# One more gate pair as block products, one gate fewer in the first phase, another order of units and of the steps at the border

## The chip, the cores and the metric

The kernel runs on one core of a Trainium2 chip. The metric is the device time of one execution in microseconds. The engines are named as in the profile: PE (TensorE, matmuls), PEld (its weight loads), DVE (VectorE), ACT (ScalarE), POOL (GpSimd), SP (SyncE, which issues the DMAs). Each engine works through a queue of its own; semaphores order them among one another.

## What is computed

One layer of a hybrid encoder on 1040 tokens (16 meta tokens and 1024 of the input) of width 1024, all in float32. The part that the change touches is the combined input projection and what follows from it:

```python
h = rmsnorm(h_res, norm1_w[l])
proj = h @ w_in[l]
(q, k, v, z, b_raw, a_raw, sc_b, sc_c, sc_x, gate_a, gate_b) = jnp.split(proj, SPLIT_POINTS, axis=-1)
o_dn = gated_deltanet_bidir(q, k, v, z, b_raw, a_raw, ...)
y_a = o_dn @ w_branch_dn[l]
y_b = (sc_b * depthwise_conv_centred(sc_c * sc_x, sc_conv_w[l])) @ w_branch_sc[l]
merged = jax.nn.sigmoid(gate_a) * y_a + jax.nn.sigmoid(gate_b) * y_b
```

`gated_deltanet_bidir` works on 8 heads: a short convolution on q, k and v, norms, for every chunk of tokens the inverse of a triangular matrix, and a scan over the chunks in both directions. A gated norm with silu(z) follows. Behind the merge come an output projection, and a SwiGLU block of width 2816.

## The kernel before

**Products.** Every float32 operand is kept as a high part (ACT copies it to the reduced type, `split`, L100 to L102) and a low part (DVE subtracts). A dense product of a 128-column unit of weights with 512 tokens is 8 blocks x 3 matmuls (high-high, high-low, low-high) = 24 matmuls of 128x512 (`dense`, L129). Where two units and two halves of the tokens are taken together, a scheme of seven block products in place of eight is used (`pair`, L1525): sums of weight blocks (`sums`, L1414) are multiplied with sums of token blocks T1 to T4 (`moving_sums`, L1442), each product being 12 matmuls (`product`, L1434).

**First phase** (L251 to L1395). The order of every engine's instructions is written out by hand: the program is traced under `tc.manual_schedule()` by a planner that keeps a modelled clock for each engine (the dictionary T). PE's base load is a sequence of *units*, each a 128-column block of the projection: q, k and v of each head (`u_qkv`), the three parts of a short-convolution block (`u_short`), gates (`u_gate`), z (`u_z`). `pick` (L973) chooses the unit two places ahead. A head's k, q, v are preferred where `qkv_ok` allows them (head h needs scan h-3 to be over; v also needs scan h-2 to have begun); otherwise the next *fill* is taken from `fill_units`: eight gates (four blocks j of gate A and gate B), five z units, then eight triples of short-convolution units. When the second or third unit of a triple is next (`mid`), it is taken whatever `qkv_ok` says. Between a unit's matmuls the planner puts in the steps of four streams: decay, norm, inverse, scan. Only one head at a time is in each stream, and the second part of an inverse and a scan hold a lock that excludes the other. DVE's convolutions, forward substitutions and norms come from three lanes (`pump`).

A scan (`g_scan`, L785) copies the values of its head into the tile vS (L808, one buffer), runs 8 steps, norms the sums in NP, and transposes them into a bank. ACT copies that into NP (L951, two buffers) and SP stores it to o_d (L953).

**Border** (L1481 to L1605). Under a second manual schedule, for DVE and PE only (L1484), come the last three z units (heads 5, 6, 7; `z_rows`, two halves of 24 matmuls each, tanh on ACT, a combination on DVE at L1495), the sums T1 to T4 in four steps of a generator (each ends with `split`, a cast by ACT and a subtraction by DVE of 128x2048), and the first pair. Instructions of a manual engine keep the written order among themselves; the framework's scheduler may put later instructions, from outside the block, between them. ACT's order, and SP's, are the scheduler's. The written order is the first part of `moving_sums`, then the weights of z6, z5's first half, and so on (the removed lines of the diff show it). The first pair's results leave their banks through ACT copies (L1534, L1546, L1548) and DVE additions (L1409 is the line of `add`), and products 3, 5 and 7 of a pair accumulate in the bank that product 1 began.

**After it** come the other three pairs, branch B's and branch A's projections, the merge, the output projection and the SwiGLU block, of which nothing is changed. The pairs' weights take two large tiles in turn (mB, mA); the p_d blocks are staged in the one that the last pair doesn't use (L1612).

Of the kernel before, what the change touches and what calls it, by code (L numbers as in the profile page):

```python
# [16 lines left out]
P = 128  # L17
# [7 lines left out]
H = 8  # L25
# [1 line left out]
FF = 2816  # L27
NF = FF // P
ZH = 5
GH = 4  # L30
EPS = 1e-6
NEG = -1e30

OQ, OK, OV, OZ, OBA, OSB, OSC, OSX, OGA, OGB = (
    0, 1024, 2048, 3072, 4096, 4128, 5152, 6176, 7200, 8224)


def unit(col):

    return (col if col < OBA else col - 32) // P  # L40
# [8 lines left out]
def encoder_layer(ctx: ExitStack, tc: tile.TileContext, x, meta, norm1_w, w_in, w_ba,  # L49
                  dn_conv_w, A_log, dt_bias, dn_norm_w, sc_conv_w, w_bdn, w_bsc,  # L50
                  w_out, norm2_w, w_gu, w_down, final_w, out):
    nc = tc.nc
# [12 lines left out]
    def uid(s):  # L65
        cnt["n"] += 1
        return f"{s}_{cnt['n']}"
# [29 lines left out]
    def transpose(dst, src, n=P):  # L97
        nc.tensor.transpose(dst, src, ident[:n, :n])

    def split(hi, lo, src):  # L100
        nc.scalar.copy(hi, src)  # L101
        nc.vector.tensor_tensor(out=lo, in0=src, in1=hi.bitcast(F32), op=ALU.subtract)  # L102
# [11 lines left out]
    def staged(shape):  # L114
        return *wtiles(shape), rawtile(shape)

    def wload(src, j):
        wh, wl, raw = staged([P, KT, P])
        nc.sync.dma_start(raw, src[j])
        split(wh, wl, raw)  # L120
        return wh, wl
# [56 lines left out]
    def sub(out, a, b):  # L178
        nc.vector.tensor_tensor(out=out, in0=a, in1=b, op=ALU.subtract)
# [91 lines left out]
    def pe(ns):  # L271
        T["pe"] += ns
        return T["pe"] + HOP

    def V(n, kind=0):
        return on("dve", (68 + 1.042 * n, 130 + 1.042 * n, 130 + 0.52 * n)[kind])

    def A(n):
        return on("act", 144 + 0.834 * n)
# [175 lines left out]
    def u_gate(j, dst, w):  # L455
        for i in range(2):
            po = psm()
            yield from dense_steps(po, w, hx, META + 512 * i, 512)
            th = half_buffer()
            nc.scalar.activation(th[:, :512], po, AF.Tanh, scale=0.5)  # L460
            A(512)
            nc.sync.dma_start(dst[:, 512 * i:512 * i + 512], th[:, :512])

    def u_z(h, w):

        rest = None
        for i in range(2):
            po = psm()
            for k, _ in enumerate(dense_steps(po, w, hx, META + 512 * i, 512)):
                if k == 11 and rest:  # L470
                    rest()
                yield
            th = half_buffer()[:, :512]
            nc.scalar.activation(th, po, AF.Tanh, scale=0.5)
            A(512)

            def rest(i=i, th=th, po=po):
                nc.vector.scalar_tensor_tensor(out=th, in0=th, scalar=1.0, in1=po, op0=ALU.add, op1=ALU.mult)
                V(512)
                nc.sync.dma_start(z_d[h][:, 512 * i:512 * i + 512], th)  # L480
        T["dve"] = max(T["dve"], T["act"] + HOP)
        rest()
# [302 lines left out]
    def g_scan(h, st_):  # L785
        nonlocal freed
        kq, vT, small, kn, NP, PQ, Pm = (st_[k] for k in ("kq", "vT", "small", "kn", "NP", "PQ", "Pm"))
# [4 lines left out]
        vS = dn.tile([P, 9, P], F32, tag="vS", name=uid("vS"))  # L792
        yield from take("scan")

        def newbank():
            return pss().rearrange("p (a n) -> p a n", a=4)
# [63 lines left out]
        for i in range(NC):  # L860
# [6 lines left out]
            t = pe(215 * len(act_))  # L867
# [5 lines left out]
            for d in act_:  # L873
# [4 lines left out]
                t = V(P, 1)  # L878
# [7 lines left out]
            for d in range(2):  # L886
# [3 lines left out]
                t = A(P)  # L890
# [5 lines left out]
            if i < NC - 1:  # L896
# [3 lines left out]
                t = pe(430)  # L900
# [3 lines left out]
            t2 = pe(430)  # L904
            if i < NC - 1:
                yield t
                for d in range(2):
# [6 lines left out]
                    t = V(P, 1)  # L914
# [28 lines left out]
            yield T["pe"] + 300  # L943
        yield T["dve"] + HOP
        for c4 in range(2):
            oT = NP[:, 4 * c4:4 * c4 + 4, 1 - c4]
            pt = newbank()
            for c in range(4):
                transpose(pt[:, c], oacc[4 * c4 + c])
            yield pe(430)  # L950
            nc.scalar.copy(oT, pt)  # L951
            A(512)
            nc.sync.dma_start(o_d[h][:, c4 * 512:(c4 + 1) * 512].rearrange("p (c t) -> p c t", c=4), oT)  # L953
# [5 lines left out]
                 for h in range(H) for i, off in enumerate((OK, OQ, OV))]  # L959
    fill_units = [(off + j * P, lambda w, j=j, i=i: u_short(j, i, w), None, i)  # L960
                  for j in range(8) for i, off in enumerate((OSC, OSX, OSB))]
    fill_units += [(off + j * P, lambda w, j=j, d_=d_[j]: u_gate(j, d_, w), None, None)
                   for j in range(GH) for off, d_ in ((OGA, ta_d), (OGB, tb_d))]
    fill_units += [(OZ + h * P, lambda w, h=h: u_z(h, w), None, None) for h in range(ZH)]
    fill_units = fill_units[24:] + fill_units[:24]
    done = freed = 0
    decs, norms, invs, scans = [], [], [], []

# [67 lines left out]
    with tc.tile_pool(name="st", bufs=1) as st:  # L1036
# [64 lines left out]
        def high(t, g):  # L1101
            p = size(t)
            nc.scalar.copy(hx[0][:, 4 * g:4 * g + 4, C0 + P * t:C0 + P * t + p], banks[t, g][:, :, :p])  # L1103
# [308 lines left out]
    mov = {}  # L1412
# [29 lines left out]
    def moving_sums():  # L1442

        c = [slice(C0 + META + 512 * i, C0 + META + 512 * i + 512) for i in range(2)]
        f = lambda m: m.bitcast(F32)
        h0, h1 = ([f(hx[0][:, 4 * i:4 * i + 4, cc]) for cc in c] for i in range(2))
        l0, l1, l2 = ([f(t[:, :, cc]) for cc in c] for t in low_tiles)
        for i in range(2):
            for j in range(2):
                mov[f"B{i + 1}{j + 1}"] = hx[0][:, 4 * i:4 * i + 4, c[j]], [hx[1][4 * i + k][:, c[j]] for k in range(4)]  # L1450
        for i, n in enumerate(("T1", "T2", "T3")):
            t = big(f"b{i}", [P, 2, 4, 512])
            mov[n] = t[:, 0], t[:, 1]
        x, y = (big(g, [P, 2, 4, 512], F32) for g in ("mA", "b3"))
        t1, t2, t3, d_ = x[:, 0], x[:, 1], y[:, 0], y[:, 1]
        a, b = slice(0, 2), slice(2, 4)
        sub(t1, h0[1], h0[0])
        sub(d_, l0[1], l0[0])
        add(t1, t1, d_)
        split(*mov["T1"], t1)  # L1460
        yield
        sub(t2, h1[1], t1)
        add(t2[:, a], t2[:, a], l1[1])
        add(t2[:, b], t2[:, b], l2[1])
        split(*mov["T2"], t2)
        yield
        sub(t3, h1[1], h0[1])
        sub(d_[:, a], l1[1], l0[1][:, a])
        sub(d_[:, b], l2[1], l0[1][:, b])
        add(t3, t3, d_)  # L1470
        split(*mov["T3"], t3)
        yield
        t = big("b3", [P, 2, 4, 512])
        mov["T4"] = t[:, 0], t[:, 1]
        sub(t1, h1[0], t2)
        add(t1[:, a], t1[:, a], l1[0])
        add(t1[:, b], t1[:, b], l2[0])
        split(*mov["T4"], t1)
        yield

    raw_slots.extend((tp, f"raw{i}") for i in range(2))  # L1481
    left, right = slice(0, 512), slice(512, 1024)
    border0 = ExitStack()
    border0.enter_context(tc.manual_schedule(engines={mybir.EngineType.DVE, mybir.EngineType.PE}))  # L1484
    z_units = [wload(w_in, unit(OZ + ZH * P))]

    def z_rows(h):
# [13 lines left out]
    def pair_weights(n, j):  # L1501

        s_hl[n % 2] = big(("mB", "mA")[n % 2], [P, 2, 2, KT, P])
        if n == 0:
            u = big("w2", [P, 2, 4, P])
            u_hl[0] = u[:, 0], u[:, 1]
        elif n == 1:
            u_hl[1] = [tp.tile([P, 4, P], F32R, tag="t2", name=uid("u_hl"), bufs=2) for _ in range(2)]
        gh, gl = wtiles([P, KT, P])
        rg, ru = (rawtile([P, KT, P]) for _ in range(2))  # L1510
        nc.sync.dma_start(rg, w_in[unit(OGA + j * P)])
        nc.sync.dma_start(ru, w_in[unit(OGB + j * P)])
        A_ = {"A11": (gh[:, 0:4], gl[:, 0:4]), "A12": (gh[:, 4:8], gl[:, 4:8])}

        def first():
            split(gh, gl, rg)

        def second():
            split(*u_hl[n % 2], ru[:, 4:8])
            A_["A22"] = u_hl[n % 2]  # L1520
            sums(rg, ru, rg[:, 0:4], rg[:, 4:8], ru[:, 0:4], ru[:, 4:8])
            stationary2(n, ru, rg, ru, A_)
        return A_, first, second

    def pair(n, j, A_, first, second):  # L1525
# [54 lines left out]
        return o1  # L1580

    sums_of_blocks = moving_sums()
    z0, z1, z2 = (z_rows(h) for h in range(ZH, H))
    next(sums_of_blocks)
    z_units.append(wload(w_in, unit(OZ + (ZH + 1) * P)))
    next(z0)
    next(z0)
    next(sums_of_blocks)
    z_units.append(wload(w_in, unit(OZ + (H - 1) * P)))
    next(z0)  # L1590
    pair0 = pair_weights(0, GH)
    next(z1)
    pair0[1]()
    next(z1)
    pair0[2]()
    next(z1)
    next(z2)
    next(sums_of_blocks)
    next(z2)
    next(sums_of_blocks)  # L1600
    next(z2)
    for n, j in enumerate(range(GH, KT)):
        o1 = pair(n, j, *(pair_weights(n, j) if n else pair0))
        if n == 0:
            border0.close()  # L1605
# [5 lines left out]
    for j in range(KT):  # L1611
        pr = mg[GH % 2 == 0][:, j] if j < 4 else s4(SEQ) if j < 6 else rawtile([P, SEQ])  # L1612
        nc.sync.dma_start(pr, p_d[j])
# [47 lines left out]
    mov = {n: (b_hl[:, 2 * i], b_hl[:, 2 * i + 1]) for i, n in enumerate(("B11", "B21"))}  # L1661
# [84 lines left out]
    t = KT - 1  # L1746
# [229 lines left out]
```

## Time and profile before

| what | value |
|---|---|
| three timed runs, median (lowest to highest) | 2003.53 us (2002.02 to 2005.52) |
| the profiled execution, its own time | 2004.27 us |
| its span, first to last instruction | 2002.5 us |
| mean granted PE clock | 0.995 |
| head 0's first chunk of values to the last head's output store | 214.0 to 951.9 us |
| last fill's last DVE instruction (L451) | 970.4 us |
| first pair's first product (L1440) | 1009.3 us |
| HBM read, written | 180.67 MB, 68.25 MB |

The page of the profile gives busy times and the costliest groups; its lists of waits say who waited for whom; the windows give each engine's busy time, the granted clock and the DMA share of a stretch; the timeline lists instructions with the idle time ahead of them in brackets and what ended it. PE's matmuls overlap in the records: a 128x512 one is shown with some 390 ns while the next starts some 227 ns later, so its cost is taken from starts.

### The profile page before, as it was taken

Reading aid. Unit: us, or ns where it says so; the run is one execution under the profiler, and the core shown is the slowest. Engines: PE = TensorE matmul, PEld = TensorE weight load, DVE = VectorE, ACT = ScalarE, POOL = GpSimd, SP = SyncE. Lnnn points to the kernel's source line nnn. Section 1 sums busy time; section 2 is a strip of 40 time slices with the busy share of each in tenths; the row PEclk is TensorE's granted clock in tenths of the full one; section 3 lists DMA queues with packets and bytes.
Section 4 is the critical chain, followed back from the end, with each engine's and each line's share of the span. In section 5 each row is a group of like instructions: output and inputs, shape, how many; then the busy total and the mean of one; then the engine's idle time right before and its main releaser. Section 6 shows DMA issues by size and latency. Waiting matters only on the chain.

```text
span 2002.5 us, 31873 instructions
## 1 busy us (share of the span) xinstructions
PE 1977.3 (99%) x12011; PEld 1724.1 (86%) x12011; DVE 1396.6 (70%) x3013; ACT 836.4 (42%) x1961; POOL 107.8 (5%) x407
## 2 busy tenths in 40 slices
PE   9999999999999999999999999999999999999998
PEld 8998889899999999999788888887878888888887
DVE  6887688878888888855685544469766666656575
ACT  6472465536463646333244221225323333334344
POOL 2011101010101010100000000000000000000000
PEclk9999999999999999999999999999999999999999
DMA  3123222222132222221236743123765345477654
GB/s 132 65 90 95 80 80 75 85 61 83 45 99 59 75 59 75 59 65 43 95 116 242 249 160 95 63 93 110 256 217 217 123 155 188 158 273 244 195 172 167
DMA packets 131121, 251.00 MB, mean 125 GB/s; under 512 B 45013, under 2 KB 54662, under 8 KB 128535
## 3 DMA queue, kind: packets, MB, share of 16 engines
q1 hardware_dynamic: 130391, 247.92, 37.5%
q8 instruction: 94, 1.54, 0.3%
q10 hardware_dynamic: 576, 1.05, 0.1%
q14 instruction: 60, 0.49, 0.1%
HBM read 180.67 MB, written 68.25 MB: 124 GB/s over the span
## 4 chain that ended last, share of the span: by engine, by line
PE 90%; DVE 4%; DMA 3%; ACT 1%; issue 1%; SPq 0%; DVEq 0%; ACTq 0%
PE pm L341 33%; PE pd L1440 12%; PE pe L1440 5%; PE pm L1440 3%; PE pd L903 1%; PE pd L882 1%; PE pd L866 1%; PE pe L136 1%; PE pe L134 1%; PE pd L869 1%; PE pe L135 1%; PE pe L603 1%; PE pd L134 1%; PE pd L136 1%; PE pd L135 1%; PE pe L1882 1%
## 5 line engine op out<-in xcount | busy, mean ns | idle before, releaser
L341 PE MATMUL pm<-hTh,wh 128*128 128x512 f32 (+4 forms) x1296 | 446.4, 350 | 0.3 <-ACT hTh L1103 0.2
L341 PE MATMUL pm<-al,wh 128*128 128x512 f32 (+4 forms) x1296 | 445.9, 349 | 0.0
L341 PE MATMUL pm<-hTh,wl 128*128 128x512 f32 (+4 forms) x1296 | 443.8, 348 | 0.0
L341 PEld LDWEIGHTS pm<-hTh,wh 128*128 128x128 f32 x1296 | 242.7, 188 | 13.7 <-issue 0.8
L341 PEld LDWEIGHTS pm<-hTh,wl 128*128 128x128 f32 x1296 | 242.9, 188 | 12.3 <-issue 0.4
L341 PEld LDWEIGHTS pm<-al,wh 128*128 128x128 f32 x1296 | 242.9, 188 | 12.2 <-issue 0.4
L102 DVE TENSOR_TENSOR al<-raw,ring_h 128x1024 fp32r<-128x1024 f32 x73 | 88.6, 1222 | 65.0 <-ACT ring_h L101 64.7
L101 ACT CAST ring_h<-raw 128x1024 fp32r<-128x1024 f32 x73 | 76.7, 1053 | 107.8 <-PE pd L1884 34.4
L990 DVE TENSOR_TENSOR wl<-raw,wh 128x512 fp32r<-128x512 f32 x118 | 79.5, 688 | 30.6 <-ACT wh L993 30.2
L363 DVE SCALAR_TENSOR_TENSOR kq<-ra,wc,kq 128x520 f32<-128x520 f32 x128 | 96.6, 755 | 4.8 <-ACT kq L393 3.5
L889 ACT ACTIVATE w<-pd,small 128x128 f32<-128x128 f32 x128 | 39.9, 363 | 117.1 <-PE pd L882 116.7
L101 ACT CAST wh<-raw 128x1024 fp32r<-128x1024 f32 x47 | 49.3, 1050 | 87.4 <-PE pe L135 25.5
L496 DVE TENSOR_TENSOR tm<-fP,fN 128x135 f32<-128x135 f32 (+23 forms) x248 | 72.0, 290 | 4.9
L500 DVE TENSOR_TENSOR fP<-fP,tm 128x135 f32<-128x135 f32 (+23 forms) x248 | 71.6, 289 | 5.1
L993 ACT CAST wh<-raw 128x512 fp32r<-128x512 f32 x118 | 69.2, 621 | 3.7 <-issue 3.6
L1409 DVE TENSOR_TENSOR b<-pd,b 128x512 f32<-128x512 f32 x22 | 15.2, 690 | 69.4 <-PE pd L1440 69.4
L1819 ACT ACTIVATE b<-b 128x512 f32<-128x512 f32 x22 | 13.9, 632 | 114.3 <-DVE b L1409 114.3
L102 DVE TENSOR_TENSOR wl<-raw,wh 128x1024 fp32r<-128x1024 f32 x47 | 57.3, 1219 | 3.8 <-ACT wh L101 3.7
L856 ACT ACTIVATE jk<-NP 128x128 f32<-128x128 f32 x64 | 19.9, 311 | 83.5 <-DVE NP L852 82.5
L876 DVE SCALAR_TENSOR_TENSOR r<-pd,negEG,vS 128x128 f32<-128x128 f32 x120 | 36.8, 345 | 25.7 <-PE pd L866 25.2
L1440 PE MATMUL pd<-b_hl,wh 128*128 128x512 f32 x176 | 54.5, 391 | 0.0
L912 DVE SCALAR_TENSOR_TENSOR S<-S,eGl,pd 128x128 f32<-128x128 f32 x104 | 31.6, 342 | 30.2 <-PE pd L899 29.8
(590 smaller groups left out, 4689.5 us busy)
## 6 DMA issues: line engine op xcount, KB each, us to landing
raw<-in_w_in_dram SPq DMA_DIRECT2D x72, 512.0 KB
raw<-in_w_gate_up_dram SPq DMA_DIRECT2D x44, 512.0 KB
sums<-in_w_down_dram SPq DMA_DIRECT2D x22, 512.0 KB
t_d<-sums SPq DMA_DIRECT2D x11, 1024.0 KB
raw<-s_d SPq DMA_DIRECT2D x44, 256.0 KB
raw<-t_d SPq DMA_DIRECT2D x44, 256.0 KB
act_d<-b SPq DMA_DIRECT2D x43, 256.0 KB
raw<-act_d SPq DMA_DIRECT2D x33, 256.0 KB
```

Of the source, the lines that this page charges most:

```text
L101: nc.scalar.copy(hi, src)
L102: nc.vector.tensor_tensor(out=lo, in0=src, in1=hi.bitcast(F32), op=ALU.subtract)
L134: mm(po[:m, :n], wh[:, k, :m], xhk[:, t0:t0 + n], start=(k == 0), stop=False)
L135: mm(po[:m, :n], wh[:, k, :m], xlk[:, t0:t0 + n], start=False, stop=False)
L136: mm(po[:m, :n], wl[:, k, :m], xhk[:, t0:t0 + n], start=False, stop=(k == KT - 1))
L341: mm(po[:, :n], ww[:, k], f(k)[:, t0:t0 + n], start=i == 0, stop=i == 3 * KT - 1)
L363: nc.vector.scalar_tensor_tensor(out=acc, in0=raw[:, h0 + t:h0 + t + hn], scalar=wc[:, t, col:col + 1], in1=acc, op0=ALU.mult, op1=ALU.add)
L496: nc.vector.tensor_tensor(out=tv, in0=fP[:, 0:r, j:j + 1].broadcast_to([P, r, n]), in1=fN[:, j:j + 1, j + 1:32].broadcast_to([P, r, n]), o ...
L500: nc.vector.tensor_tensor(out=fP[:, 0:r, j + 1:32], in0=fP[:, 0:r, j + 1:32], in1=tv, op=ALU.subtract)
L990: nc.vector.tensor_tensor(out=u[1][1][:, k], in0=u[2][:, k], in1=u[1][0][:, k].bitcast(F32), op=ALU.subtract)
L993: nc.scalar.copy(u[1][0][:, k], u[2][:, k])
L1440: mm(po, x[:, k], y, start=k + i == 0 and not add_to, stop=k == 3 and i == 2, skip_group_check=add_to)
```

## The change

1. `GH` goes from 4 to 3: gate block 3 (two units) leaves the fills, and five pairs are taken by the seven products.
2. The fills come in another order: three gates, the eight triples, the other three gates, the five z units.
3. A scan's transposed output is copied into vS and stored from there.
4. At the border ACT joins the engines in written order; the sums' four steps become seven, in which the low part of a sum is taken one step after its cast; z6's weights are loaded and split ahead of the first sum, and the other steps are put in other places.

```diff
@@ -27,7 +27,7 @@
 FF = 2816
 NF = FF // P
 ZH = 5
-GH = 4
+GH = 3
 EPS = 1e-6
 NEG = -1e30
 
@@ -943,7 +943,7 @@
             yield T["pe"] + 300
         yield T["dve"] + HOP
         for c4 in range(2):
-            oT = NP[:, 4 * c4:4 * c4 + 4, 1 - c4]
+            oT = vS[:, 4 * c4:4 * c4 + 4]
             pt = newbank()
             for c in range(4):
                 transpose(pt[:, c], oacc[4 * c4 + c])
@@ -962,7 +962,7 @@
     fill_units += [(off + j * P, lambda w, j=j, d_=d_[j]: u_gate(j, d_, w), None, None)
                    for j in range(GH) for off, d_ in ((OGA, ta_d), (OGB, tb_d))]
     fill_units += [(OZ + h * P, lambda w, h=h: u_z(h, w), None, None) for h in range(ZH)]
-    fill_units = fill_units[24:] + fill_units[:24]
+    fill_units = fill_units[24:24 + 3] + fill_units[:24] + fill_units[24 + 3:]
     done = freed = 0
     decs, norms, invs, scans = [], [], [], []
 
@@ -1454,34 +1454,43 @@
         x, y = (big(g, [P, 2, 4, 512], F32) for g in ("mA", "b3"))
         t1, t2, t3, d_ = x[:, 0], x[:, 1], y[:, 0], y[:, 1]
         a, b = slice(0, 2), slice(2, 4)
+        high = lambda n, t: nc.scalar.copy(mov[n][0], t)
+        low_part = lambda n, t: sub(mov[n][1], t, f(mov[n][0]))
         sub(t1, h0[1], h0[0])
         sub(d_, l0[1], l0[0])
         add(t1, t1, d_)
-        split(*mov["T1"], t1)
+        high("T1", t1)
         yield
         sub(t2, h1[1], t1)
         add(t2[:, a], t2[:, a], l1[1])
         add(t2[:, b], t2[:, b], l2[1])
-        split(*mov["T2"], t2)
+        high("T2", t2)
+        low_part("T1", t1)
+        yield
+        low_part("T2", t2)
         yield
         sub(t3, h1[1], h0[1])
         sub(d_[:, a], l1[1], l0[1][:, a])
         sub(d_[:, b], l2[1], l0[1][:, b])
         add(t3, t3, d_)
-        split(*mov["T3"], t3)
+        high("T3", t3)
+        yield
+        sub(t1, h1[0], t2)
+        low_part("T3", t3)
         yield
         t = big("b3", [P, 2, 4, 512])
         mov["T4"] = t[:, 0], t[:, 1]
-        sub(t1, h1[0], t2)
         add(t1[:, a], t1[:, a], l1[0])
         add(t1[:, b], t1[:, b], l2[0])
-        split(*mov["T4"], t1)
+        high("T4", t1)
+        yield
+        low_part("T4", t1)
         yield
 
     raw_slots.extend((tp, f"raw{i}") for i in range(2))
     left, right = slice(0, 512), slice(512, 1024)
     border0 = ExitStack()
-    border0.enter_context(tc.manual_schedule(engines={mybir.EngineType.DVE, mybir.EngineType.PE}))
+    border0.enter_context(tc.manual_schedule(engines={mybir.EngineType.DVE, mybir.EngineType.PE, mybir.EngineType.Activation}))
     z_units = [wload(w_in, unit(OZ + ZH * P))]
 
     def z_rows(h):
@@ -1581,24 +1590,27 @@
 
     sums_of_blocks = moving_sums()
     z0, z1, z2 = (z_rows(h) for h in range(ZH, H))
-    next(sums_of_blocks)
     z_units.append(wload(w_in, unit(OZ + (ZH + 1) * P)))
     next(z0)
+    next(sums_of_blocks)
+    next(sums_of_blocks)
     next(z0)
+    z_units.append(wload(w_in, unit(OZ + (H - 1) * P)))
     next(sums_of_blocks)
-    z_units.append(wload(w_in, unit(OZ + (H - 1) * P)))
     next(z0)
+    next(z1)
     pair0 = pair_weights(0, GH)
     next(z1)
     pair0[1]()
     next(z1)
     pair0[2]()
-    next(z1)
     next(z2)
     next(sums_of_blocks)
     next(z2)
     next(sums_of_blocks)
+    next(sums_of_blocks)
     next(z2)
+    next(sums_of_blocks)
     for n, j in enumerate(range(GH, KT)):
         o1 = pair(n, j, *(pair_weights(n, j) if n else pair0))
         if n == 0:
```

## The prediction

> **What bounds the kernel now.** First the head of the page, then the list of what TensorE (PE) waited for.
>
> ```profile
> span 2002.5 us, 31873 instructions
> PE 1977.3 (99%) x12011; PEld 1724.1 (86%) x12011; DVE 1396.6 (70%) x3013; ACT 836.4 (42%) x1961; POOL 107.8 (5%) x407
> PE 90%; DVE 4%; DMA 3%; ACT 1%; issue 1%; SPq 0%; DVEq 0%; ACTq 0%
> PE pe L136 <- DVE wl L102: 3.8, 1, 3.8
> ```
>
> PE is the bound: the chain that ended last runs over it for 90% of the span, and its longest single wait anywhere is 3.8 us. So only two things pay: fewer PE instructions, and holes closed. The one big hole lies where the diff works, between the first phase and the gate pairs. The chain of waits there, in order of time (start, us, what):
>
> ```profile
> 971.10 2.02 DMA p_d<-rb
> 973.24 2.29 DVE mA L179
> ...
> 980.09 1.92 ACT b L101
> 982.03 2.29 DVE b L102
> 984.32 1.15 DVE wl L102
> 985.51 0.79 PE pe L136
> 986.30 0.43 PE pe L134
> ...
> 990.88 0.23 PE pe L136
> ```
>
> The low part of head 6's z weights (984.32) stands in DVE's queue behind the three passes of T1, ACT's cast and the low part of T1. PE had started 48 matmuls of z5 at about 970.2 and two of z6, was through at 981.5, and stood until 985.51: 4.0 us. Then twelve matmuls took 0.43 us instead of 0.23, another 2.5 us. The hole costs **6.5 us**. The windows show the granted clock (the 0.50) in that stretch:
>
> ```profile
> 987.00:988.00 1.00, 1.00 (x4) 0.81 (x3) 1.00 (x1) 0.00 (x0) 0.00 (x0) 0.50 0.96 381
> ```
>
> **The change part by part.** Costs of matmuls, from a stretch that holds two gate units and nothing else, and one that holds 512-wide products throughout:
>
> ```profile
> 170.90:192.60 21.70, 21.70 (x97) 17.97 (x96) 1.00 0.30 102
> 1100.00:1200.00 100.00, 100.00 (x443) 82.81 (x442) 47.46 (x51) 20.74 (x20) 0.00 (x0) 1.00 0.59 202
> ```
>
> (a) *Three gates for four, five pairs for four.* Two dense units of 48 matmuls leave the first phase: 96 x 0.226 = -21.7 us. A fifth pair of seven products of 12 comes: 84 x 0.226 = +19.0 us. Net **-2.7 us**, if PE stays the bound on both sides. Weight loads (2 x 512 KB), stores, and the casts move from the first phase to the pairs, where DVE is busy for 47 of 100 us in the row above: hidden there. The fifth pair ends in the other large tile (mB), so the staging of p_d moves to mA, which is free as early: nothing.
>
> (b) *z weights ahead of the sums.* The low part of z6 now goes to DVE right after the last fill unit, some 2 us after z0 starts on PE, and is wanted 10.9 us after it. The hole above goes: **-6.5 us**.
>
> (c) *ACT in the written order, casts and low parts of the sums staggered.* What is late next? In before, DVE and PE follow the written order here and ACT does not:
>
> ```profile
> 1012.25 0.59 ACT L1534 COPY s<-pd 128x512 f32<-128x512 f32 x1 [1.36 <-PE pd L1440]
> ...
> 1018.23 1.92 ACT L101 CAST b<-b 128x2048 fp32r<-128x2048 f32 x1
> ```
>
> The copy at 1012.25 is written in `pair`, behind all seven steps of the sums, but ACT took it ahead of the cast of T3 (1018.23), and of T4's later still. What a written order does to such an instruction is seen on DVE:
>
> ```profile
> 1029.97 2.29 DVE L102 TENSOR_TENSOR b<-mA,b 128x2048 fp32r<-128x2048 f32 x1 [2.03 <-ACT b L101]
> ...
> 1032.77 0.68 DVE L1409 TENSOR_TENSOR s<-pm,s 128x512 f32<-128x512 f32 x1
> ```
>
> The addition at 1032.77 reads the first pair's second product (bank pm), which PE had done by 1014.8 (the rows of products below); it came 18 us later, behind the low part of T4. With ACT in the written order the copy of the first pair's first bank comes behind T4's cast, and PE's third product of that pair accumulates into the same bank, so PE waits for the copy. When? Count from z0's first matmul (0). DVE can begin T1 at about 4.0 (973.24 - 970.2 = 3.0 in before; the last fill is now a z unit, with a tanh of 0.6 ahead of its DVE pass and store). Two rows give the shorter passes (two of 1024, three of 512):
>
> ```profile
> 988.29 2.36 DVE L1409 TENSOR_TENSOR mA<-mA,al 128x1024 f32<-128x1024 f32 x2
> ...
> 1003.70 1.89 DVE L179 TENSOR_TENSOR raw<-raw,raw 128x512 f32<-128x512 f32 x3
> ```
>
> Up to T4's sum DVE has 10 passes of 2048 at 2.25, 6 of 1024 additions at 1.18, 4 low parts of 1024 at 1.15 and 10 instructions of 512 at 0.63: 22.5 + 7.1 + 4.6 + 6.3 = 40.5 us. So T4's sum is ready at 44.5, or 47.5 with three waits of about 1 us (z7's cast, a cast of the first pair's sums, one low part of the next pair's weights slipped in). Cast 1.9, copy 0.6: the bank is free at 47.0 to 50.0. PE ends six z halves at 6 x 24 x 0.227 = 32.7 and the two products ahead of the wait at 38.1. That leaves a gap of 8.9 to 11.9 us, which only products of later pairs, outside the written order, can fill. Before has such fillers:
>
> ```profile
> L1440 PE MATMUL pd<-hTh,wh x4: 389/389/389, 1009.3 to 1011.4; 128*128 128x512 f32 x4
> L1440 PE MATMUL pm<-hTh,wl x4: 389/389/389, 1012.5 to 1014.5; 128*128 128x512 f32 x4
> L1440 PE MATMUL pe<-hTh,wh x4: 388/389/395, 1020.5 to 1022.6; 128*128 128x512 f32 x4
> ```
>
> The first two rows are the first pair's own first products; the third, in another bank, is a product of the second pair pulled ahead of the first pair's T3 product. Now two such products (5.4 us) have their weights and banks in time; a third needs a low part that DVE reaches only at about 48. Left: 3.5 to 6.5 us, taken as 4.5, and 2.5 us of slow clock as in the hole above: **+7.0 us**. Its ends: 0 (four fillers, 10.9 us, cover it) and 15 (none, 11.9, and 3.4 of slow clock). In the row nearest to this wait, the 4.0 us hole, the price was 6.5, so the middle is taken.
>
> The Trainium skill, "TensorE: Matmul & The Clock Gate", section "What's actually happening", says the half rate sets in after at least one idle window of about 3.4 us; by that a new gap under 3.4 us would cost no clock, and at its lower end (+3.5) the sum would be -5.7. This trace does not hold to it: a wait of 2.05 us was also followed by the half clock.
>
> ```profile
> 1494.67 2.85 PE L1440 MATMUL pd<-b,w 128*128 128x512 f32 x8 [2.05 <-DVE b L1409]
> ```
>
> ```profile
> 1496.00:1497.00 1.00, 1.00 (x4) 0.78 (x3) 0.61 (x1) 0.00 (x0) 0.00 (x0) 0.50 0.97 393
> ```
>
> (d) *Outputs sent from vS.* vS has one buffer, so ACT's L808 of the next head now waits for the two stores; NP is free earlier.
>
> ```profile
> 883.07 1.28 SPq L953 DMA_DIRECT2D o_d<-NP  x2
> 892.85 2.35 ACT L808 ACTIVATE vS<-pd,small 16x128 f32<-16x128 f32 x9 [1.50 <-PE pd L98]
>   DMA o_d<-NP: 1.4, 1
> ```
>
> The next write comes 8.5 us after the last store was issued, and a 256 KB store took 2.0 us (971.10 above): no wait. The 1.4 us is DVE's only wait for these stores, and PE did not stop for it. **0** on the path; bounds -1.4 and, if a scan followed at once, +2.
>
> (e) *Order of the fills.* Same work, other places: the 8 x 3 short-convolution units now follow three gate units, and three gates and five z units come last. On a busy PE this is 0. It matters only through the scans, which must be over before the fills are.
>
> ```profile
> 951.20 1.12 SPq L953 DMA_DIRECT2D o_d<-NP  x2
> 492.31 2.35 ACT L808 ACTIVATE vS<-pd,small 16x128 f32<-16x128 f32 x9 [0.70 <-PE pd L98]
> 494.57 0.24 ACT L580 COPY kn<-pe 16x128 f32<-16x128 f32 x1
> 524.52 0.34 SPq L671 DMA_DIRECT2D nd<-NP  x1
> L392 ACT COPY ra<-pm x9: 403/439/481, 453.5 to 490.6; 128x336 f32<-128x336 f32 x3, 128x320 f32<-128x320 f32 x3, 128x384 f32<-128x384 f32 x3
> ```
>
> Fills went on for 19 us after the last head's output (951.2 to 970.2); with 21.7 us less of them they would end at 948.5, 2.7 us before it. So the cover is just gone unless the scans move. I think they move forward. Inversions run one at a time and set the pace; the inverse of head 4 could start only at 524.5, though scan 3, which follows the inverse of head 3, began at 492.3, because its normalisation (494.57) waited for head 4's q and k units, and these (453.5 on) had to let the first short triple finish. Put into the slots of before, the new list gives head 3's k one unit later (some 10 us, which the inversion lane still absorbs) and head 4's k one unit earlier, so that everything from head 4 on comes some 14 us earlier: last output near 937, fills until 948.5, cost **0**.
>
> Sum on the profiled execution (2004.27 us, span 2002.5): -2.7 - 6.5 + 7.0 + 0 + 0 = **-2.2 us**. The median of the three timed runs is 2003.53, so the forecast is 2001.3 us.
>
> **Rivals.** *The new ACT order costs little.* If DVE has no waits and four products are pulled ahead, PE stands for 0 to 2 us and the clock stays up: -2.7 - 6.5 + 1 = -8.2, 1995.3 us. For it: before filled the whole wait for T4 that way. Against: weights and banks for a third filler come late. *The change doesn't do what it says for PE:* no filler fits, and the gap of 11.9 + 3.4 comes whole: -9.2 + 15 = +5.8, 2009.3 us. Against: the filler row. *The scans outlast the fills (slower).* Place: the end of the first phase. A head's k may be chosen only between triples; if a scan ends just after that choice, q and k come three units, about 50 us, late. By my estimate from the starts of the units and scans in the trace, the choices for heads 4 to 7 follow the end of the scan they need by 18, 13, 16 and 9 us; one miss puts the last output at about 937 + 35 = 972 instead of 937, and PE then has 20 us of scan with half of it idle, and a slow clock: about +15 on -2.2, 2016 us. It decides from the moment the last output comes after 948.5.
>
> **How the numbers follow.** Forecast (1998.5 to 2005) 40%; cheap ACT order 28%; scans outlast the fills 22%; no fillers 10%. 0.2% is 4 us, about what a measurement can tell from no change: faster is below 1999.5, slower above 2007.5. Faster takes the 28% and a quarter of the forecast's 40%: 38%. Slower takes the last two cases, less their milder part: 29%. Same: 33%. The range, 1994 to 2012, leaves out the worse half of the scan case and the tails. The likeliest case's own range is 1998.5 to 2005.
>
> **What would show it.** The wait of L136 for L102 near z6 gone; 1200 instead of 1296 matmuls in each L341 group. Right on (c): a wait of PE in L1440 for ACT's L1534 some 40 to 50 us after z0, with a stretch of clock 0.50 behind it; wrong: products back to back through the first pair. Right on (e): the last o_d store before the last fill's evictions. Wrong: PE waiting on scan lines (L866 to L903) or L98 at the end of the first phase. What would break the forecast most is (e), since its slots are taken from the old timing.

## The result and the profile after

The changed kernel takes 2007.28 us (median of 22 runs, 2003.46 to 2011.47) against 2003.41 us before (22 runs beside them, 2000.47 to 2006.41): ratio 1.0018, 95% interval 1.0012 to 1.0025. That is slower by about 3.9 us, just inside the 0.2% that the prediction took for no difference, and on the other side of 1 than its forecast of 2001.3. The profiled execution is the fastest of the 22: 2003.46 us, span 2001.7. So a second profile of the same kernel was taken (the last of the experiments, span 2004.7); both are read here.

The head of the page of the first profile:

```profile
span 2001.7 us, 31862 instructions
PE 1974.2 (99%) x11999; PEld 1720.7 (86%) x11999; DVE 1398.8 (70%) x3020; ACT 837.2 (42%) x1964; POOL 108.0 (5%) x407
```

Cut at the start of z0 (the first L134 matmul behind the fills) and at the first L134 matmul of branch B behind the pairs, with 0.227 us for each of the 144 matmuls of the z units and the 84 of each pair that lie between them:

| | z0 starts | z0 to branch B | of it matmuls | of it holes and slow clock | branch B to the end |
|---|---|---|---|---|---|
| before | 970.2 | 115.9 | 480 x 0.227 = 109.0 | 6.9 | 916.4 |
| after | 946.0 | 142.7 | 564 x 0.227 = 128.0 | 14.7 | 913.0 |
| after, second profile | 946.6 | 144.8 | 128.0 | 16.8 | 913.3 |

The first phase became 24 us shorter, the fifth pair costs 19, and **the holes of the border doubled**. What PE waited for, from the list of waits (total, times, longest):

```profile
PE pd L1440 <- DVE s L1504: 7.7, 2, 5.9
...
PE pd L1440 <- ACT s L1543: 1.1, 1, 1.1
...
PE pd L136 <- DVE wl L102: 0.5, 1, 0.5
```

The wait of 3.8 us for z6's low part (L136 for L102) is gone; the 0.5 in the last row is for z7's. In its place stands a larger one, in the first pair. PE's timeline there (start, duration, line; in brackets the idle time ahead and what ended it):

```profile
985.12 0.39 PE L1440 MATMUL pm<-hTh,wl 128*128 128x512 f32 x1
991.38 0.77 PE L1440 MATMUL pd<-hTh,wh 128*128 128x512 f32 x1 [5.88 <-DVE s L1504]
...
996.21 0.50 PE L1440 MATMUL pd<-hTh,wl 128*128 128x512 f32 x1
998.56 0.50 PE L1440 MATMUL pd<-hTh,wh 128*128 128x512 f32 x1 [1.85 <-DVE s L1504]
998.90 0.40 PE L1440 MATMUL pd<-al,wh 128*128 128x512 f32 x1
1000.43 2.93 PE L1440 MATMUL pd<-b,mB 128*128 128x512 f32 x6 [1.14 <-ACT s L1543]
```

At 985.12 the first pair's second product ends. Its third (operands b and mB, the sums) starts at 1000.43, when ACT's copy has freed the bank. In the 15 us between them PE ran one product of a later pair (twelve matmuls, 991.38 to 996.21) and two matmuls of another. Each of these had to wait for a bank that a z unit's combination on DVE (L1504, z2's two halves) gave back. ACT, in the same stretch:

```profile
981.29 0.59 ACT L1502 ACTIVATE s<-pd 128x512 f32<-128x512 f32 x1
...
990.67 1.90 ACT L1457 CAST b<-b 128x2048 fp32r<-128x2048 f32 x1 [4.09 <-DVE b L1409]
992.48 0.59 ACT L1502 ACTIVATE s<-pd 128x512 f32<-128x512 f32 x1
998.00 1.90 ACT L1457 CAST b<-mA 128x2048 fp32r<-128x2048 f32 x1 [4.93 <-DVE mA L1409]
999.81 0.58 ACT L1543 COPY s<-pd 128x512 f32<-128x512 f32 x1
```

ACT is idle for 4.09 and 4.93 us, waiting for the sums of T3 and T4, and behind their casts stand, in the written order, z2's second tanh (992.48) and the copy of the first pair's bank (999.81; ready to run since that bank's product ended). z2's first tanh had run at 981.29. DVE, whose sums make ACT wait:

```profile
953.10 2.29 DVE L179 TENSOR_TENSOR mA<-hTh 128x2048 f32<-128x2048 f32 x1 [4.26 <-issue]
...
990.55 0.68 DVE L1504 SCALAR_TENSOR_TENSOR s<-s,pd 128x512 f32<-128x512 f32 x1
...
995.55 2.35 DVE L1409 TENSOR_TENSOR mA<-mA,al 128x1024 f32<-128x1024 f32 x2
997.83 0.68 DVE L1504 SCALAR_TENSOR_TENSOR s<-s,pd 128x512 f32<-128x512 f32 x1
...
999.03 1.22 DVE L102 TENSOR_TENSOR wl<-raw,wh 128x1024 fp32r<-128x1024 f32 x1
```

T1 begins at 953.10, 7.1 us after z0, and from there DVE has hardly a gap until T4's last addition (995.55 to 997.9). So PE, through ACT's order, hangs on the whole chain of the sums. The two combinations (990.55 and 997.83) stand behind the sums of T3 and T4 in DVE's own written order. The clock went with it (PEclk is the third figure from the end):

```profile
991.40:996.60 5.20, 5.20 (x12) 3.75 (x12) 5.20 (x3) 1.67 (x2) 0.00 (x0) 0.52 0.00 0
...
1000.40:1004.00 3.60, 3.56 (x10) 2.85 (x11) 3.60 (x4) 1.52 (x2) 0.00 (x0) 0.60 0.06 24
```

The end of the first phase, by line:

```profile
L953 SPq DMA_DIRECT2D o_d<-vS x4: 320/380/428, 861.6 to 938.0; - x4
```

```profile
L341 PE MATMUL pm<-hTh,wh x1264: 302/334/582, 17.6 to 945.3; 128*128 128x320 f32 x47, 128*128 128x384 f32 x45, 128*128 128x512 f32 x43, 128*128 128x336 f32 x29
```

The last head's output is stored at 938.0, and the fills go on to 945.3: the scans kept their cover.

### The profile page after: what moved, and what is told of

The parts are those of the page before. It is cut to its first block, busy times and chain, and to the rows that moved or that the text cites. A ratio compares the mean times of both kernels' runs of the same rounds, so it can differ in the third digit from the quotient of the medians.

```text
span 2001.7 us, 31862 instructions
## 1 busy us (share of the span) xinstructions
PE 1974.2 (99%) x11999; PEld 1720.7 (86%) x11999; DVE 1398.8 (70%) x3020; ACT 837.2 (42%) x1964; POOL 108.0 (5%) x407
## 4 chain that ended last, share of the span: by engine, by line
PE 47%; DVE 3%; ACT 1%; issue 1%; DMA 1%; SPq 0%; DVEq 0%; ACTq 0%
PE pd L1440 13%; PE pe L1440 6%; PE pm L1440 4%; PE pe L1894 1%; PE pe L1895 1%; PE pe L1896 1%; PE pd L1894 1%; PE pd L1895 1%; PE pd L1896 1%; PE pd L135 1%; PE pd L134 1%; PE pe L135 1%; PE pe L134 1%; PE pd L136 1%; PE pe L136 1%; PE pm L1895 1%
## 5 line engine op out<-in xcount | busy, mean ns | idle before, releaser
L341 PE MATMUL pm<-hTh,wh 128*128 128x320 f32 (+4 forms) x1264 | 434.2, 349 | 0.4 <-ACT hTh L1103 0.2
L341 PE MATMUL pm<-al,wh 128*128 128x320 f32 (+4 forms) x1264 | 433.6, 348 | 0.0
L341 PE MATMUL pm<-hTh,wl 128*128 128x320 f32 (+4 forms) x1264 | 431.7, 347 | 0.0
L341 PEld LDWEIGHTS pm<-hTh,wh 128*128 128x128 f32 x1264 | 236.7, 188 | 12.6 <-issue 1.3
L341 PEld LDWEIGHTS pm<-hTh,wl 128*128 128x128 f32 x1264 | 237.0, 188 | 10.9 <-issue 0.4
L341 PEld LDWEIGHTS pm<-al,wh 128*128 128x128 f32 x1264 | 236.9, 188 | 10.3
L102 DVE TENSOR_TENSOR al<-raw,ring_h 128x1024 fp32r<-128x1024 f32 x73 | 88.6, 1223 | 64.8 <-ACT ring_h L101 64.4
L102 DVE TENSOR_TENSOR wl<-raw,wh 128x1024 fp32r<-128x1024 f32 x48 | 58.5, 1220 | 13.6 <-ACT wh L101 13.4
L1440 PE MATMUL pd<-b_hl,wh 128*128 128x512 f32 x176 | 54.4, 390 | 0.0
L1440 PE MATMUL pd<-b,mB 128*128 128x512 f32 x204 | 50.7, 398 | 1.1 <-ACT s L1543 1.1
```

The lines of the kernel that those rows point to most:

```text
L341: mm(po[:, :n], ww[:, k], f(k)[:, t0:t0 + n], start=i == 0, stop=i == 3 * KT - 1)
L1440: mm(po, x[:, k], y, start=k + i == 0 and not add_to, stop=k == 3 and i == 2, skip_group_check=add_to)
```

## The experiments

The theory at the start (A): putting ACT into the written order costs what the rest of the change gains, because the first pair's bank copy stands behind T4's cast. The rival (B): the steps' new places on DVE, or the shorter first phase, make the hole, and ACT's order matters little. Each kernel is compared with runs of the kernel before on the same chip; the medians of before lay between 2003.4 and 2004.1 throughout.

**ACT out of the written order, all else as changed.**

```diff
-    ...manual_schedule(engines={...DVE, ...PE, mybir.EngineType.Activation}))
+    ...manual_schedule(engines={...DVE, ...PE}))
```

> The changed kernel with one edit: ACT is taken out of the engines in written order at the border (DVE and PE stay). Theory A (ACT's written order puts the first pair's copy L1543 behind T4's cast, and PE's wait for it costs about 15 us): the hole at z0 + 39 to 55 us shrinks to 4 us or less, time about 1996 us, 11 us under the changed kernel and some 7 under the kernel before. Theory B (the hole comes from DVE's written order: the z7 combinations L1504 stand behind T3 and T4 and hold the banks that the pulled-ahead products need): ACT's order is immaterial, the hole stays, about 2007 us.

Measured: 1993.76 us (1989.33 to 1996.87), ratio 0.9949 (0.9935 to 0.9962). z0 to branch B took 129.2 us: 1.2 of holes instead of 14.7. ACT's timeline shows the copy pulled ahead of both casts:

```profile
984.06 0.59 ACT L1543 COPY s<-pd 128x512 f32<-128x512 f32 x1 [0.94 <-PE pd L1440]
...
991.92 1.92 ACT L1457 CAST b<-b 128x2048 fp32r<-128x2048 f32 x1 [1.84 <-DVE b L1409]
...
999.25 1.92 ACT L1457 CAST b<-mA 128x2048 fp32r<-128x2048 f32 x1 [2.81 <-DVE mA L1409]
```

T4's cast is as late as in the changed kernel (z0 + 51.6 against z0 + 52.0), so DVE's chain is the same; only the pair's copies moved, the first from z0 + 53.8 to z0 + 36.4, and PE hardly stopped. A holds. This version is also the fastest of all: 0.5% under the kernel before.

**The other way round: the kernel before with ACT in the written order, nothing else.**

```diff
-    ...manual_schedule(engines={...DVE, ...PE}))
+    ...manual_schedule(engines={...DVE, ...PE, mybir.EngineType.Activation}))
```

> The kernel before with one edit: ACT joins the engines in written order at the border. Theory A: a second hole opens in the first pair, 10 to 15 us, since T4's cast comes later there than in the changed kernel (z0 + 58): about 2014 to 2019 us. Theory B: no new hole, 2003.5 us.

Measured: 2019.15 us (2017.19 to 2020.16), ratio 1.0075 (1.0062 to 1.0089): +15 us from one word. The wait, and ACT:

```profile
PE pd L1440 <- DVE s L1495: 8.6, 1, 8.6
```

```profile
1028.36 1.90 ACT L101 CAST b<-mA 128x2048 fp32r<-128x2048 f32 x1 [7.40 <-DVE mA L1409]
1030.16 0.58 ACT L1534 COPY s<-pd 128x512 f32<-128x512 f32 x1
```

The copy that stood at 1012.25 in before comes at 1030.16, and the fillers wait for z2's bank (L1495 is before's L1504). The same mechanism without any other part of the change.

**ACT in written order up to the first pair, free from there on.**

```diff
     next(sums_of_blocks)
+    border0.close()
+    border0.enter_context(tc.manual_schedule(engines={...DVE, ...PE}))
     for n, j in enumerate(range(GH, KT)):
```

> The changed kernel, with ACT in written order up to the first pair and free from there on (DVE and PE stay in written order throughout). It parts two readings of the gain from freeing ACT. If the place of the pair's copies behind T4's cast is what cost (theory A): about 1994 us, like the kernel with ACT free. If it was the written order among the z and sums steps themselves: about 2007 us, like the changed kernel.

Measured: 1996.34 us (1995.4 to 1997.72), ratio 0.9961 (0.9948 to 0.9973). Of the 0.69% between the changed kernel and the one with a free ACT, 0.57% come back by freeing ACT from the pair on alone. The rest is within the two intervals; in this profile PE has a gap of 3.03 us, 2.56 of them waiting, and slow clock behind it:

```profile
995.68 2.93 PE L1440 MATMUL pd<-b,mB 128*128 128x512 f32 x6 [2.56 <-DVE b L179]
```

```profile
995.70:999.40 3.70, 3.70 (x10) 2.97 (x11) 2.80 (x3) 1.41 (x1) 0.00 (x0) 0.58 0.02 9
```

**z2 earlier, ACT in written order.** The banks that the fillers waited for are given back before T3's sum:

```diff
     next(z2)
-    next(sums_of_blocks)
     next(z2)
+    next(z2)
     next(sums_of_blocks)
     next(sums_of_blocks)
-    next(z2)
+    next(sums_of_blocks)
     next(sums_of_blocks)
```

> The changed kernel with one difference: all three steps of z2 (head 7) are written ahead of T3, so that its two combinations on DVE and its tanh on ACT come earlier and its banks are given back some 8 us sooner; ACT keeps the written order, so the first pair's copy still stands behind T4's cast, at about z0 + 54. Theory A (the copy's place behind T4's cast makes the hole, the banks held by z2's combinations decide how many products of later pairs can fill it): two to three of them (5.4 to 8 us) run while PE waits, the holes between z0 and branch B shrink from 14.8 to 6 to 10 us, and the time is 1999 to 2004 us against 2004 of the kernel before. Rival B (the banks were the whole cause): no hole is left, about 1994 us. Rival C (weights, not banks, kept the fillers out): as the changed kernel, 2007 us.

Measured: 2006.71 us (2005.22 to 2008.01), ratio 1.0015 (1.0006 to 1.0024): rival C, and the theory's figure was wrong. The waits for L1504 are gone, and in their place stand the low parts of the next pairs' weights; in this order a row of PE's list of waits, of DVE's timeline and two of PE's:

```profile
PE pd L1440 <- DVE wl L102: 8.8, 2, 6.5
```

```profile
1000.20 1.22 DVE L102 TENSOR_TENSOR wl<-raw,wh 128x1024 fp32r<-128x1024 f32 x1
```

```profile
994.60 0.39 PE L1440 MATMUL pd<-hTh,wl 128*128 128x512 f32 x1
1001.47 0.80 PE L1440 MATMUL pd<-hTh,wl 128*128 128x512 f32 x1 [6.47 <-DVE wl L102]
```

The low part at 1000.20 stands in DVE's queue behind T4's additions; in the changed kernel it stood at 999.03. So two things kept the fillers out, banks and weights, both behind the sums on DVE, and freeing the banks shows the weights. One product and two matmuls ran in the hole either way.

**The border alone** (new border and ACT's order; four gates, the old fills and outputs).

```diff
-GH = 3
+GH = 4
-            oT = vS[:, 4 * c4:4 * c4 + 4]
+            oT = NP[:, 4 * c4:4 * c4 + 4, 1 - c4]
-    fill_units = fill_units[24:24 + 3] + fill_units[:24] + fill_units[24 + 3:]
+    fill_units = fill_units[24:] + fill_units[:24]
```

> The changed kernel's border alone (z weights in front, staggered sums, ACT in written order), with four gates, the old order of fills and outputs through NP. Theories A and B: the old hole of 6.5 us goes and one of about 15 comes: 2003.5 + 8.3 = 2011.8 us. If the loss of the changed kernel sat in the first phase: about 2003 us or less.

Measured: 2010.97 us (2008.48 to 2013.04), ratio 1.0034 (1.0022 to 1.0047), +6.9 us. Holes between z0 and branch B: 120.9 - 109.0 = 11.9 us, against 6.9 in before, with two waits for L1504 again:

```profile
PE pd L1440 <- DVE s L1504: 5.8, 2, 4.1
```

So the border loses 6.9 us by itself, whatever the first phase does.

**The fills alone** (three gates, five pairs, the new order of units, on the kernel before).

```diff
-GH = 4
+GH = 3
-    fill_units = fill_units[24:] + fill_units[:24]
+    fill_units = fill_units[24:24 + 3] + fill_units[:24] + fill_units[24 + 3:]
```

> The kernel before with three gates, five pairs and the new order of fills alone; border and outputs as before. By the profile of the changed kernel the first phase ends 24.2 us earlier and a pair costs 19.0: 2003.5 - 5.2 = 1998.3 us. Rival (the scans outlast the fills in typical runs, though not in the profiled one): 2004 us or more.

Measured: 2001.52 us (1999.0 to 2003.76), ratio 0.9988 (0.9979 to 0.9997): -2.5 us. This is 3 us less than was expected. z0 starts at 946.6, 23.6 us earlier, but T1 begins at z0 + 4.4 instead of 3.1, and the old hole grew:

```profile
PE pe L136 <- DVE wl L102: 5.7, 1, 5.7
```

**z6's weights ahead of the first sum, alone**, on the kernel before:

```diff
-    next(sums_of_blocks)
     z_units.append(wload(w_in, unit(OZ + (ZH + 1) * P)))
+    next(sums_of_blocks)
     next(z0)
```

> The kernel before with z6's weights loaded and split ahead of the first sum, and nothing else. The 6.5 us of the old hole go: 1997 us. Rival: T4 comes 1 us later and PE's wait moves into the first pair: 2000 us or more.

Measured: 2000.85 us (1999.22 to 2002.41), ratio 0.9981 (0.9972 to 0.9989): -3.3 us, half of the 6.5. The hole moved to z7's weights, for which PE waits until 995.9:

```profile
PE pd L136 <- DVE wl L102: 2.4, 1, 2.4
```

**Fills and z6's weights, without the staggered sums**, ACT free (the last two diffs together):

> The kernel with the new fills (three gates, five pairs), plus z6's weights ahead of the first sum; the sums in four steps with cast and low part together, ACT free, outputs through NP. If staggering the sums is worth nothing once the weights come first: 2001.5 - 9.3 (its hole of 6.1 and some 3 of slow clock) = 1992 us, level with the kernel with ACT free. If the staggering is needed: 1996 us or more.

Measured: 2001.06 us (1999.31 to 2005.76), ratio 0.9988 (0.9979 to 0.9997). Here the whole hole went to z7's weights:

```profile
PE pd L136 <- DVE wl L102: 6.9, 1, 6.9
```

The kernel with a free ACT is 7.3 us faster than this one. That is what the seven staggered steps are worth, together with the new places of the steps around them, which no run takes apart (the outputs from vS, the other difference, are worth nothing, below). Here DVE waits 1.98 and 1.96 us for the casts of T1 and T2, and z7's low part stands behind T2's, 20.4 us after T1's start. With the staggered steps and a free ACT it stands ahead of T2's low part, DVE doesn't wait for these casts, and it comes 14.3 us after T1's start.

**The outputs from vS alone**, on the kernel before:

```diff
-            oT = NP[:, 4 * c4:4 * c4 + 4, 1 - c4]
+            oT = vS[:, 4 * c4:4 * c4 + 4]
```

> The kernel before with the scans' outputs sent from vS, and nothing else. The prediction's 0: 2003.5 to 2004 us, no PE wait for L808 and no DVE wait for the stores of o_d. Rival (the next head's copies wait for the stores): a microsecond or two per head, 2008 us or more.

Measured: 2003.89 us (2002.6 to 2007.19), ratio 1.0004 (0.9995 to 1.0013). Nothing, as expected.

**A gate pair more** (six pairs, two gates, ACT free).

```diff
-GH = 3
+GH = 2
```

> The changed kernel with ACT taken out of the written order and one gate pair more (two gates in the first phase, six pairs). Two gate units of 48 matmuls leave the first phase (-21.7 us) and 84 come to the pairs (+19.0). Theory: the fills are also the cover of the scans. With three gates the last head's output was stored some 9 us ahead of the last fill's end; with 21.7 us less the fills end near 925, the scans near 938, and PE stands half idle for some 13 us and gets the slow clock behind it: 1993.8 - 2.7 + 8 to 20 = 1999 to 2011 us, with PE waiting on the scan's lines. Rival (the scans move forward with the fills, or other work covers them): 1993.8 - 2.7 = 1991 us and no such waits.

Measured: 1997.92 us (1996.32 to 2000.09), ratio 0.9971 (0.9959 to 0.9982): 0.2% slower than with three gates, a little under the theory's range, and by another way. PE did not stand in the scan's end: the last fill ended at 920, z0 started at 921.9 among the last scan's steps and filled them; only 0.3 us of wait is left there. The price came later. The chain of waits, DVE, and PE's list:

```profile
934.24 1.98 DMA o_d<-vS
```

```profile
936.53 2.29 DVE L179 TENSOR_TENSOR mA<-hTh 128x2048 f32<-128x2048 f32 x1 [3.33 <-DMA o_d<-vS]
...
950.79 1.22 DVE L102 TENSOR_TENSOR wl<-raw,wh 128x1024 fp32r<-128x1024 f32 x1
```

```profile
PE pd L136 <- DVE wl L102: 5.1, 1, 5.1
```

T1 had to wait for the last output's store, so the sums began 14.6 us after z0, and z7's weights behind them came late.

**The changed kernel once more.**

> The changed kernel once more, unaltered, for a second profile: the first profile was of the fastest of its executions. If the new hole is the cause, it stands again between z0 and branch B with 14 to 16 us in all, the first pair's copy comes some 54 us after z0 behind T4's cast, and the difference between the first profile (2003.5 us) and the median (2007.3 us) is slow clock behind short gaps elsewhere, in spells of 3.4 us, which come in some executions and not in others. Rival: the hole itself varies by several us from execution to execution.

Measured: 2005.40 us (2003.89 to 2008.07, 8 runs), ratio 1.0010 (1.0000 to 1.0020). The waits in the first pair are the same:

```profile
PE pd L1440 <- DVE s L1504: 7.8, 2, 5.9
...
PE pd L1440 <- ACT s L1543: 1.1, 1, 1.1
```

The two spans differ by 3.0 us: 0.6 of it arises before z0, 2.0 between z0 and branch B, 0.4 behind. In two stretches the slow clock differs; first the first profile, then the second:

```profile
986.00:1008.00 22.00, 13.63 (x41) 10.24 (x42) 20.01 (x17) 8.93 (x10) 0.00 (x0) 0.77 0.14 53
1384.00:1404.00 20.00, 16.54 (x62) 11.80 (x61) 18.11 (x23) 8.37 (x10) 0.00 (x0) 0.91 0.49 159
```

```profile
986.00:1008.00 22.00, 13.05 (x33) 9.39 (x33) 19.94 (x17) 8.28 (x9) 0.00 (x0) 0.69 0.16 58
1384.00:1404.00 20.00, 16.86 (x58) 11.89 (x57) 18.20 (x21) 6.75 (x8) 0.00 (x0) 0.83 0.49 161
```

Time under the half clock is 2 x (1 - PEclk) x length: 10.1 and 3.6 us in the first, 13.6 and 6.8 us in the second, one spell of some 3.4 us more in each stretch. A spell does half the work of its length, so it costs up to 1.7 us. In the first stretch it cost 1.5: the same matmul comes 1.15 us later in the second profile ahead of it, 2.65 behind it. In the second stretch it cost 0.8, of which 0.7 are gone again by 1406, where the first profile alone has a wait for DVE (0.50). So the rival (a hole that varies by several us) falls, but only some half of the 3.0 us is shown to be slow clock.

## Why the prediction was wrong

By its own steps:

- **(a) Fills and fifth pair, -2.7: right, and a little more.** The first phase became 24.2 us shorter (23.6 in the second profile and with the fills alone, 22.5 with a free ACT) where 96 x 0.226 = 21.7 was reckoned; the 0.8 to 2.5 us beyond that were not traced. One figure was a slip: the 96 matmuls are spread over three L341 groups, so each loses 32 (1264), not 96.
- **(b) The old hole, -6.5: right in place; it depends on the staggering.** z6's wait is gone in the changed kernel, and 0.5 us is left for z7's. But the early weights alone gave 3.3 us, and nothing together with the new fills, because z7's weights are next in DVE's queue. The prediction did not ask what is late behind z6; the seven steps, for which it reckoned with no gain, are what closes the hole.
- **(c) ACT in the written order, +7.0: the step that failed.** The mechanism is the one that was written down, the first pair's copy behind T4's cast, and both runs that move only ACT's order show it (-14 and +15 us). Its size was not. All holes together were put at 6.9 - 6.5 + 7.0 = 7.4 us; they are 14.7 and 16.8. In the first profile PE's three waits in the first pair are 8.9 us where 4.5 was taken, and the slow clock took another 3.9 (0.52 over 5.2 us and 0.60 over 3.6) where 2.5 was taken. The wait was too small for two reasons. *The copy*: the bank was to be free at z0 + 47.0 to 50.0, it was at z0 + 54.4. T1 began at z0 + 7.1 instead of 4.0, and DVE took 44.8 us from there to T4's sum instead of 40.5 to 43.5: it did 13 instructions of 512 columns and five low parts of 1024 in that time, where 10 and four were counted. *The fillers*: "two such products (5.4 us) have their weights and banks in time" was wrong. One came in, late and under the half clock, and two matmuls. The row shown for it, a product of the second pair in bank pe, is of the old kernel, in which the first pair was not held up. In the changed kernel the fillers' banks came from z2's combinations, at z0 + 44.6 and 51.9. DVE's written order holds these, not ACT's: with a free ACT they come at z0 + 44.2 and 51.4. And with the banks given back early, the weights' low part held the fillers up just as long.
- **(d) Outputs from vS, 0: right**, by the run that does it alone.
- **(e) Order of the fills, 0: right.** The last output was stored at 938.0 (937 was forecast), 7 us ahead of the last fill matmul. But the price put on a miss was told wrongly: with two gates the fills end before the scans, PE does not stand there, since z0 slides in, and the loss is that T1 waits for the last store. The new order also has a price at the border, the z unit's store ahead of T1, which is in (c).

Of the rivals, "no filler fits" (holes of +15, 2009.3 us) had the right size of the hole and got a tenth of the chance; it lies 2 us above the measurement, about what the first phase gained beyond the sum. The size is in part luck: it reckoned with a gap of 11.9 us and no filler, and the gap was 15.1 us with a filler and two matmuls in it. "Cheap ACT order" fell: four fillers were never there. The sum without (c), -9.2, is near what the version with a free ACT shows: -10.3.

That the whole sum missed by less than its term (c) is luck too. In the two profiles the holes lie 7.3 and 9.4 us above the forecast, the spans 1.4 and 4.4, because two gains that no term held hide the rest: about 2 us in the first phase, and 3 us behind branch B's start.

These 3 us stay open. Before's wait of 2.05 us near 1494 and the slow clock behind it are missing in the first profile of after, and 0.2 us of the wait are there in the second, while the kernel with a free ACT has the wait again (2.1 us) without a slow clock. None of the runs tells why the wait comes and goes, and neither forecast nor hole rests on it.

Why T1 began at z0 + 7.1 the traces show. DVE's queue stands ahead of it until 952.96, on the semaphore of the last z unit's store, which SP issued at 948.88, 0.6 us behind a 512 KB load. In six profiles with a load there (both of after, ACT free, ACT free from the pair on, z2 earlier, fills with z6's weights) T1 begins 4.2 to 4.8 us after the issue of that last store; in four without one (before, the border, the fills and z6's weights each alone) it begins 2.1 us after it. From the fills alone to the fills with z6's weights, T1 goes from z0 + 4.4 to z0 + 7.6: the early weights of (b) bring the load ahead of the store.

## What to carry to other kernels

Putting an engine into a written order makes every instruction on it wait for whatever is written ahead: look for the short instruction that frees another engine's buffer (here a copy of 0.58 us) and ask which long chain now stands before it. When a gap is to be filled by work pulled ahead, work out the fillers' banks and weights under the new order; rows of the old kernel show fillers under the old order, in banks that the new one may not give them. And when a late operand is moved ahead, look at once for the next late one: here z7 took over z6's wait, until the long steps were cut in pieces.

## What the runs showed of the hardware

The slow clock comes in spells of some 3.4 us, and the same wait may bring one, two or none. The same wait of 2.6 us, in the two profiles of the changed kernel:

```profile
1387.97 0.50 PE L1440 MATMUL pd<-b,w 128*128 128x512 f32 x1 [2.61 <-ACT b L101]
```

```profile
1390.59 0.79 PE L1440 MATMUL pd<-b,w 128*128 128x512 f32 x1 [2.60 <-ACT b L101]
```

It was followed by one spell and by two (the windows above). A wait of 2.56 us was followed by one spell (ACT free from the pair on, rows above); one of 2.41 us by none, in the kernel with z6's weights ahead of the first sum:

```profile
995.88 0.50 PE L136 MATMUL pd<-hTh,wl 128*128 128x512 f32 x1 [2.41 <-DVE wl L102]
```

```profile
996.00:1000.00 4.00, 4.00 (x18) 3.27 (x19) 3.93 (x6) 0.00 (x0) 0.00 (x0) 1.00 0.79 226
```

What tells these waits apart stands in the clock records of the traces. In each profile all spells begin on one grid with a step of 3.413 us: in the first profile of after they begin at 989.62, 999.86 and 1388.97, which is 3 and 114 steps apart. Now add up PE's idle time, by its matmul records, within each step. From 60 us on, the 13 profiles have some 7290 steps under the full clock; a spell began behind each of the 33 with 1.88 us of idle or more, and behind none with 1.85 or less. The wait of 2.41 us lies across a grid point, 1.20 us in one step and 1.21 in the next. Before's wait of 2.05 us lies whole in one step (1492.38 to 1495.80), and a spell began at its end. So what counts is how much idle time one step collects, not the length of a wait alone.

The Trainium skill, "TensorE: Matmul & The Clock Gate", section "What's actually happening", has the clock fall to half after at least one idle window of about 3.4 us, and calls that window free-running. The grid and the length of the spells agree with a free-running window; that a whole window must be idle does not agree with the 1.88 us that were enough here.

Where a wait falls on the grid differs from execution to execution. The two profiles of the changed kernel have the same waits in the first pair, and there the clock alone makes 1.5 us between them; so a single profile of this kernel can lie off the median without any long wait being different.
